# FFN activations turned in 32x32 blocks on VectorE and placed through DRAM, for ten of eleven blocks

## The chip, the cores and the metric

One NeuronCore of a Trainium2 chip runs the whole program. The metric is the device time of one execution in microseconds (us). A core has a tensor engine (PE, with its weight loads PEld), VectorE (DVE), ScalarE (ACT), GpSimd (POOL) and SyncE (SP), which here issues every DMA. Each engine takes its instructions in the order in which they were written for it, and waits at the first one that is not ready.

## The reference

The reference is a two-layer decoder trunk on 256 tokens of 1024 features, in float32. In each layer a feed-forward network (FFN) stands before and behind a mixer, so there are four FFNs:

```python
def swiglu(h, w_gate, w_up, w_down):
    return (jax.nn.silu(h @ w_gate) * (h @ w_up)) @ w_down

def rms_norm(x, gain):
    xf = x.astype(jnp.float32)
    y = xf * lax.rsqrt(jnp.mean(xf * xf, axis=-1, keepdims=True) + RMS_EPS)
    return (y * gain.astype(jnp.float32)).astype(x.dtype)

for layer in range(DEPTH):
    x = x + 0.5 * swiglu(rms_norm(x, ffn1_norm[layer]), ffn1_w_gate[layer], ffn1_w_up[layer], ffn1_w_down[layer])
    h = rms_norm(x, mix_norm[layer])
...
    x = x + mix
    x = x + 0.5 * swiglu(rms_norm(x, ffn2_norm[layer]), ffn2_w_gate[layer], ffn2_w_up[layer], ffn2_w_down[layer])
...
```

w_gate and w_up are 1024 x 2816, w_down is 2816 x 1024. The mixer of layer 0 is an mLSTM beside cross-attention to a memory, that of layer 1 a dilated attention beside the same; between the layers one projection makes the keys and values that layer 1 uses. The change touches the FFNs alone.

## The kernel before

**Numbers.** Each float32 matrix is held as two float32r parts, hi (rounded) and lo (what that leaves), and each product is three matmuls (`mm3`, lines 555 to 560): the low part of the weights by the high part of the activations first, then high by high, then high weights by the low part of the activations.

**Weights.** They come as one stream of units of [128, 1024] floats (512 KB), in the order of use. SP loads a unit into one of six tiles `raw`; ACT rounds it to `hi` (1024 columns); DVE subtracts to get `lo`; both go into a ring of eight units. So the load of unit i waits for the `lo` of unit i-6 (line 499), and the `hi` of unit i waits until PE has done with unit i-8 (line 508). In the names below raw221 is unit 221.

**An FFN** (`ffn`, lines 720 to 783) cuts the 2816 hidden features into eleven blocks of 256 (b = 0 to 10), and the tokens into two tiles of 128 (t = 0, 1). `gu(b, t)` multiplies the tokens by four units of gate and up weights: 24 matmuls of 512 columns into a bank of PSUM, `gups`. Each quarter of them uses one unit, and the unit's place in the ring is free when the same quarter of t = 1 is done. Then a side chain, `hidden(b, t)`, makes the activations: `sil` on ACT, `h` [128 tokens, 256] on DVE, two transposes on PE (128x128 each, by an identity, into the PSUM tile `tph`), `hh` on ACT and `hl` on DVE (hi and lo of the transposed tile). `dn(b, t)` multiplies `hh`, `hl` by two units of down weights, 12 matmuls, into four banks `acc` that stay open over all blocks.

**The order.** PE runs gu(0,0), gu(0,1), gu(1,0), gu(1,1), dn(0,0), dn(0,1), gu(2,0), gu(2,1), dn(1,0), dn(1,1) and so on, one block behind, up to dn(7); the end is gu(9,0), gu(9,1), gu(10,0), dn(8,0), gu(10,1), dn(9,0), dn(10,0), dn(8,1), dn(9,1), dn(10,1). This main stream is fixed by the loops. Where the side chains and the splits of the weights are put between it, on PE, ACT, DVE and SP, is decided when the program is written out: `_Model` (lines 168 to 263) keeps a clock for each engine by rough costs, and a chain's next step is written when that clock says that its inputs are ready. The costs are constants of the code, for a DMA a time by size and 2.0 us until it lands. On the chip the written order is all that is left of this.

Of the kernel before, what the change touches and what calls it, by code (L numbers as in the profile page):

```python
# [8 lines left out]
F32 = mybir.dt.float32  # L9
# [8 lines left out]
P = 128  # L18
# [4 lines left out]
NB = FF // FB  # L23
EPS = 1e-6
# [19 lines left out]
def kper(layer, which, b):  # L44
    return 1 if (layer, which, b) == (0, 1, 0) else 2


def _stream():
    """The weights in the order in which they are used: (key, source, slices, width)."""
# [64 lines left out]
def _pack(units, w):  # L114
    """Lay the weights out as one flat array, unit after unit, [128, width] each."""
    parts = []
    for _, src, _ in units:
        if src is None:
            continue
        name, index, cols, k, n = src  # L120
        if cols is None:
            a = w[name][index] if index is not None else w[name]
            parts.append(a[k * P:(k + 1) * P, :].reshape(-1))
# [18 lines left out]
def _consts():  # L142
    """Constants of the shapes alone: identity, triangle, ones, selectors, T5 buckets, masks."""
# [122 lines left out]
class _Engine:  # L266
    """An engine of the core whose instructions the model follows."""
# [57 lines left out]
class _Chain:  # L325
    """A chain of steps that is emitted beside the main stream, each when the one before is done."""
# [6 lines left out]
class _Kernel:  # L333
# [74 lines left out]
    def until(self, t):  # L408
        """run the chains that are ready before the main stream can go on at t"""
# [19 lines left out]
    def wait(self, *chains):  # L429
        """in a chain: until others are done"""  # L430
# [5 lines left out]
    def when(self, *aps):  # L436
        """in a chain: until something is written"""
# [3 lines left out]
    def psum(self, pool, shape, name):  # L441
        """in a chain: a bank of PSUM, once no more than can be are held by chains"""
# [30 lines left out]
    def emit_unit(self):  # L473
        """the next unit's steps begin: hi, the weights in float32r, and lo, what that leaves"""
# [24 lines left out]
    def loads(self):  # L499
        """loads run as far ahead of the splits as there are tiles"""  # L500
# [7 lines left out]
    def unit_ready(self):  # L508
        """when the split of the next unit can begin without delaying other work"""
# [57 lines left out]
    def rpow(self, ss, n, scale):  # L567
        """(ss * scale + eps) ** -0.5, [128, n]"""
# [7 lines left out]
    def rms(self, src, out, later=LATER):  # L576
        """out [128, 1] = 1 / rms of each row of src [128, 1024]"""
# [12 lines left out]
    def transposed(self, src, hi, lo, chunks, gain=None):  # L590
        """hi, lo [128, 8, 128] take the transposed 128-column chunks of src, times the gain"""
# [46 lines left out]
    def head_norm(self, src, n, out, rstd):  # L638
        """out = src * rstd normed over groups of 64; src [128, n*64] in PSUM"""
# [29 lines left out]
    def memory_load(self, layer):  # L669
        """the memory, ahead of its use"""  # L670
# [18 lines left out]
    def project(self, ps, x, key, n, kper):  # L689
        """ps [128, n] = xT.T @ weights of the block; x is xT or the number of a tile of tokens"""  # L690
# [13 lines left out]
    def block(self, x, key, n, kper, after):  # L704
        """a block of n columns of a projection; after(ps) are the steps that take it on"""
# [13 lines left out]

    def ffn(self, layer, which, after):  # L720
        nc = self.nc
        acc = [[self.acc.tile([P, 512], F32, tag="acc", name=f"acc{t}{h}") for h in range(2)]
               for t in range(2)]
        chains, hT = {}, {}

        def hidden(b, t):
            def steps(ps):
                yield from self.wait(self.stats[t])
                rstd = self.rstd[t]
                sil = self.work.tile([P, FB], F32, tag="ta", bufs=4, name="sil")  # L730
                nc.scalar.activation(sil, ps[:, :FB], AF.Silu, scale=rstd)
                yield
                h = self.work.tile([P, FB], F32, tag="ta", bufs=4, name="h")
                nc.vector.scalar_tensor_tensor(h, ps[:, FB:], rstd, sil, ALU.mult, ALU.mult)
                yield FREE
# [8 lines left out]
                hT[b, t] = (hh, hl)  # L744
            return steps

        def gu(b, t):
            chains[b, t] = self.block(t, ("gu", layer, which, b), 512, kper(layer, which, b), hidden(b, t))

        def dn(b, t):  # L750
            self.finish(chains.pop((b, t)))
            hh, hl = hT.pop((b, t))
# [3 lines left out]
            for n, (c, h) in enumerate(pairs):  # L756
                wh, wl = self.get("dn", layer, which, b, c)
                self.until(max(self.model.ready(a) for a in (wl, hl)))
                s = slice(c * P, (c + 1) * P)
                f = slice(h * 512, (h + 1) * 512)  # L760
                self.mm3(acc[t][h], (hh[:, s], hl[:, s]), (wh[:, f], wl[:, f]),
# [106 lines left out]
    def out_part(self, key, t, acc, haT, order, chunks, after=None):  # L868
        """some chunks of an output projection; the last ones end with the residual"""
# [21 lines left out]

    def mixer_a(self, after):
        nc, io = self.nc, self.io
        with ExitStack() as ctx:
# [44 lines left out]
            def gates():  # L939
                # u = i - cumsum(log sigmoid f), cg = max(0, running max of u)  # L940
# [210 lines left out]

    def shared_kv(self, again):
# [298 lines left out]
```

## Time and profile before

| what | value |
|---|---|
| median of three timed runs | 1037.3 us (1035.68 to 1037.99) |
| profiled execution, first to last instruction (span) | 1036.0 us |
| PE busy | 1019.0 us, 98% of the span |
| DVE busy, ACT busy | 616.1 us (59%), 557.5 us (54%) |
| moved by DMA | 182.53 MB, the main queue busy 52.0% |
| transposes of FFN activations (`tph`) | 176, 272 ns each |

The profiled execution is told by its span alone; the timed runs are executions of their own, and their median is 1.3 us above it. In the views, L545 is a matmul of the helper `matmul`, L552 a transpose, and L276 stands for every instruction of the other engines. Times in a row are us from the start of the span. `<-` behind an idle time names what ended it. A matmul's duration (about 390 ns) overlaps the next one's; the time that it costs is the distance from start to start.

### The profile page before, as it was taken

How to read it: one execution, taken by the hardware profiler on the slowest of the kernel's cores; microseconds unless marked ns; L12 is line 12 of the kernel's file. 1: busy time of each engine (PE TensorE's matmuls, PEld its weight loads, DVE VectorE, ACT ScalarE, POOL GpSimd, SP SyncE). 2: the span in 40 equal slices, each digit the busy share in tenths (PEclk: the TensorE clock that was granted, in tenths of full speed). 3: DMA queues.
4: the chain of work that ended last, by engine and by line, in shares of the span. 5: the costliest groups of instructions: out<-in, count | busy, mean ns of one | idle time of the engine just before them, and what ended most of it. 6: DMA issues, size and time to landing. Idle time of an engine off the chain costs nothing.

```text
span 1036.0 us, 13199 instructions
## 1 busy us (share of the span) xinstructions
PE 1019.0 (98%) x4888; PEld 840.4 (81%) x4888; DVE 616.1 (59%) x903; ACT 557.5 (54%) x913; POOL 43.7 (4%) x78
## 2 busy tenths in 40 slices
PE   7999999999999999999999999999999999999998
PEld 5888888898888888888877888888887688888886
DVE  6655554767866755554565755455476865545452
ACT  7544453596775744454466644445366774545441
POOL 0000000111110000000011000000003000000000
PEclk9999999999999999999999999999999999999999
DMA  8764644553537465656454656464552246555531
GB/s 292 246 212 166 214 166 152 169 196 103 185 104 241 146 215 169 209 166 211 164 188 163 208 199 207 167 214 166 181 198 68 82 167 218 170 198 184 182 121 41
DMA packets 54329, 182.53 MB, mean 176 GB/s; under 512 B 6332, under 2 KB 8180, under 8 KB 54264
## 3 DMA queue, kind: packets, MB, share of 16 engines
q1 hardware_dynamic: 54264, 181.69, 52.0%
q8 instruction: 38, 0.62, 0.2%
q14 instruction: 27, 0.22, 0.1%
HBM read 180.60 MB, written 1.07 MB: 175 GB/s over the span
## 4 chain that ended last, share of the span: by engine, by line
PE 92%; DVE 3%; ACT 2%; DMA 1%; issue 1%; POOL 0%; SPq 0%; DVEq 0%; ACTq 0%
PE gups L545 47%; PE acc L545 23%; PE aps L545 6%; PE oacc L545 3%; PE bqps L545 2%; PE mkvps L545 2%; PE kvps L545 2%; PE tph L552 2%; PE tps L552 2%; DVE lo L276 1%; DMA raw<-in_wts 1%; PE sc L545 1%; DVE s L276 1%; PE ms L545 1%; PE po L545 0%
## 5 line engine op out<-in xcount | busy, mean ns | idle before, releaser
L276 DVE TENSOR_TENSOR lo<-raw,hi 128x1024 fp32r<-128x1024 f32 (+3 forms) x347 | 404.1, 1184 | 152.0 <-ACT hi L276 137.2
L276 ACT CAST hi<-raw 128x1024 fp32r<-128x1024 f32 (+3 forms) x347 | 349.3, 1021 | 110.7 <-PE acc L545 66.0
L545 PE MATMUL gups<-lo,xh 128*128 128x512 f32 x704 | 280.9, 399 | 1.3 <-DVE lo L276 1.3
L545 PE MATMUL gups<-hi,xl 128*128 128x512 f32 x704 | 275.8, 392 | 0.0
L545 PE MATMUL gups<-hi,xh 128*128 128x512 f32 x704 | 275.1, 391 | 0.0
L545 PEld LDWEIGHTS gups<-hi,xl 128*128 128x128 f32 x704 | 132.6, 188 | 28.5
L545 PEld LDWEIGHTS gups<-lo,xh 128*128 128x128 f32 x704 | 132.6, 188 | 28.5 <-DVE lo L276 2.9
L545 PEld LDWEIGHTS gups<-hi,xh 128*128 128x128 f32 x704 | 133.0, 189 | 25.9
L545 PE MATMUL acc<-lo,hh 128*128 128x512 f32 x352 | 141.8, 403 | 0.0
L545 PE MATMUL acc<-hi,hl 128*128 128x512 f32 x352 | 138.0, 392 | 0.0
L276 ACT ACTIVATE sil<-gups,rstd 128x256 f32<-128x256 f32 x88 | 41.8, 475 | 178.3 <-PE gups L545 178.3
L545 PE MATMUL acc<-hi,hh 128*128 128x512 f32 x352 | 137.2, 390 | 0.0
L276 DVE SCALAR_TENSOR_TENSOR h<-gups,rstd,sil 128x256 f32<-128x256 f32 x88 | 42.3, 481 | 140.9 <-ACT sil L276 140.9
L545 PEld LDWEIGHTS acc<-hi,hl 128*128 128x128 f32 x352 | 66.1, 188 | 14.5
L545 PEld LDWEIGHTS acc<-hi,hh 128*128 128x128 f32 x352 | 66.4, 189 | 12.6
L276 ACT CAST hh<-tph 128x256 fp32r<-128x256 f32 x88 | 32.8, 372 | 80.9 <-PE tph L552 80.9
L545 PEld LDWEIGHTS acc<-lo,hh 128*128 128x128 f32 x352 | 66.2, 188 | 12.2
L276 DVE TENSOR_TENSOR hl<-tph,hh 128x256 fp32r<-128x256 f32 x88 | 37.4, 425 | 39.7 <-ACT hh L276 39.7
L545 PE MATMUL aps<-lo,xh 128*128 128x384 f32 (+1 forms) x144 | 49.8, 346 | 0.0
L545 PE MATMUL aps<-hi,xl 128*128 128x384 f32 (+1 forms) x144 | 47.6, 330 | 0.0
L545 PE MATMUL aps<-hi,xh 128*128 128x384 f32 (+1 forms) x144 | 47.5, 330 | 0.0
L276 ACT ACTIVATE xh<-tps,gains 128x128 fp32r<-128x128 f32 x112 | 31.9, 373 | 24.8 <-PE tps L552 24.8
(176 smaller groups left out, 932.8 us busy)
## 6 DMA issues: line engine op xcount, KB each, us to landing
raw<-in_wts SPq DMA_DIRECT2D x304, 512.0 KB, 4.6
raw<-in_wts SPq DMA_DIRECT2D x32, 384.0 KB, 3.6
raw<-in_wts SPq DMA_DIRECT2D x8, 256.0 KB, 4.6
mt<-in_mem SPq DMA_DIRECT2D x4, 512.0 KB, 5.8
bias<-diag SPq DMA_DIRECT2D x1, 1536.0 KB, 8.0
x<-in_x SPq DMA_DIRECT2D x4, 256.0 KB, 3.6
out<-x SPq DMA_DIRECT2D x4, 256.0 KB, 2.0
raw<-in_wts SPq DMA_DIRECT2D x2, 396.0 KB, 3.5
```

Of the source, the lines that this page charges most:

```text
L276: call(out, *args, **kw)
L545: self.pe.matmul(out, lhsT=lhsT, rhs=rhs, start=start, stop=stop)
L552: self.pe.transpose(out, in_, ident)
```

## The change

For blocks 0 to 9 of each FFN (`TURNED = NB - 1` is 10) the activations are no longer transposed on PE. DVE turns `h` [128, 256] (made as before, by `activated`) in 32x32 blocks with one instruction for each t, into a tile `hb` [128, 512] that holds both token tiles. When both are there, SP writes `hb` to a DRAM tile `hd` (256 KB, runs of 2 KB), and reads it back as `ht` [128, 512], with four runs of 512 bytes for each partition, so that each 32x32 block lands where the full transpose has it. One ACT instruction and one DVE instruction, 512 columns each, split `ht` into `hhb` and `hlb`, in place of two of 256 columns each. The features land on the partitions in another order (32 j + r on 4 r + j), and the rows of the down weights of these blocks are laid out in that order on the host. Block 10 stays on PE.

```diff
+TURNED = NB - 1
     def dn(b):
         for c in range(2):
-            units.append((("dn", layer, which, b, c), (d, layer, None, 2 * b + c, 1), D))
+            rows = "turned" if b < TURNED else None
+            units.append((("dn", layer, which, b, c), (d, layer, rows, 2 * b + c, 1), D))
...
+            if cols:
+                a = a.reshape(4, 32, -1).transpose(1, 0, 2)
...
+    def hidden_blocks(b, t):
+        def steps(ps):
+            h = self.work.tile([P, FB], F32, tag="ta", bufs=4, name="h")
+            yield from activated(ps, t, h)
+            if t == 0:
+                blocks[b] = fp.tile([P, 4, 2, 2, 32], F32, tag="hb", bufs=2, name="hb")
+            nc.vector.transpose(blocks[b][:, :, :, t, :].rearrange("p j c t -> p c j t"),
+                                h.rearrange("p (c j e) -> p c j e", c=2, j=4))
+        return steps
+
+    def placed(b, before):
+        yield from self.wait(*before)
+        hb = blocks.pop(b)
+        d = self.dram.tile([P, 512], F32, tag="hd", bufs=3, name="hd")
+        nc.sync.dma_start(d, hb.rearrange("p j c t e -> p (j c t e)"))
+        yield
+        ht = fp.tile([P, 4, P], F32, tag="ht", bufs=2, name="ht")
+        nc.sync.dma_start(ht, bass.AP(d.tensor, d.offset, [[P, P], [32 * 512, 4], [1, P]]))
+        yield
+        hh = fp.tile([P, 4, 4, 32], F32R, tag="hh", bufs=3, name="hhb")
+        hl = fp.tile([P, 4, 4, 32], F32R, tag="hl", bufs=3, name="hlb")
+        yield from self.split(*(a.rearrange("p c i e -> p i c e") for a in (hh, hl)),
+                              ht.rearrange("p i (c e) -> p i c e", c=4))
...
     def gu(b, t):
-        chains[b, t] = self.block(t, ("gu", layer, which, b), 512, kper(layer, which, b), hidden(b, t))
+        steps = hidden_blocks if b < TURNED else hidden
+        chains[b, t] = self.block(t, ("gu", layer, which, b), 512, kper(layer, which, b),
+                                  steps(b, t))
+        if b < TURNED and t == 1:
+            chains[b, 0] = chains[b, 1] = self.spawn(placed(b, [chains[b, 0], chains[b, 1]]))
```

The matmuls and their order on PE stay; 160 of the 176 transposes `tph` are gone from between them. The change also moves what the planner writes around them.

SP's queue in the third FFN (layer 1, first), where block 0 is handed over; before, it holds weight loads alone:

```order
L276 DMA raw220_5497<-in_wts 128x1024
L276 DMA raw221_5552<-in_wts 128x1024
L276 DMA raw222_5561<-in_wts 128x1024
L276 DMA raw223_5573<-in_wts 128x1024
L276 DMA raw224_5592<-in_wts 128x1024
```

The same place with the change (hd_5449 and ht_5497 are the write and the read of block 0, hd_5519 and ht_5546 those of block 1):

```order
L281 DMA raw220_5443<-in_wts 128x1024
L281 DMA hd_5449<-hb_5402 128x512
L281 DMA raw221_5486<-in_wts 128x1024
L281 DMA ht_5497<-hd_5449 128x4x128
L281 DMA raw222_5500<-in_wts 128x1024
L281 DMA raw223_5512<-in_wts 128x1024
L281 DMA hd_5519<-hb_5474 128x512
L281 DMA raw224_5529<-in_wts 128x1024
L281 DMA ht_5546<-hd_5519 128x4x128
```

The read of block 0 stands behind the load of unit 221, which waits for the `lo` of unit 215. The second and the fourth FFN have the same rows there. From the third block on, the write follows the load that the `lo` behind `h` frees, and two weight loads stand between write and read.

ACT's queue at that place before, from `sil` of gu(0,1) to the splits behind `sil` of gu(1,1):

```order
L276 ACTIVATE sil_5479<-gups_5421,rstd_4826 128x256
L276 CAST hi214_5485<-raw214_5404 128x1024
L276 CAST hh_5502<-tph_5499 128x256
L276 ACTIVATE sil_5521<-gups_5481,rstd_4734 128x256
L276 CAST hh_5535<-tph_5532 128x256
L276 CAST hi215_5538<-raw215_5426 128x1024
L276 CAST hi216_5554<-raw216_5432 128x1024
L276 CAST hi217_5566<-raw217_5446 128x1024
L276 ACTIVATE sil_5575<-gups_5523,rstd_4826 128x256
L276 CAST hi218_5580<-raw218_5464 128x1024
```

ACT's queue there with the change:

```order
L281 ACTIVATE sil_5426<-gups_5373,rstd_4773 128x256
L281 CAST hi214_5436<-raw214_5355 128x1024
L281 ACTIVATE sil_5464<-gups_5428,rstd_4681 128x256
L281 CAST hi215_5479<-raw215_5378 128x1024
L281 CAST hi216_5491<-raw216_5384 128x1024
L281 CAST hi217_5505<-raw217_5397 128x1024
L281 ACTIVATE sil_5515<-gups_5466,rstd_4773 128x256
L281 CAST hhb_5521<-ht_5497 128x4x4x32
L281 CAST hi218_5525<-raw218_5411 128x1024
```

The two `hh` of block 0 stood ahead of hi215; the one `hhb` of block 0 stands behind the last `sil` of block 1. Unit 215 takes the ring place of unit 207, the first unit of gu(1).

SP's queue in the first FFN before, at the same stage:

```order
L276 DMA raw20_362<-in_wts 128x1024
L276 DMA raw21_384<-in_wts 128x1024
L276 DMA raw22_413<-in_wts 128x1024
L276 DMA raw23_426<-in_wts 128x1024
L276 DMA raw24_438<-in_wts 128x1024
L276 DMA raw25_457<-in_wts 128x1024
```

And with the change:

```order
L281 DMA raw20_360<-in_wts 128x1024
L281 DMA hd_363<-hb_283 128x512
L281 DMA raw21_378<-in_wts 128x1024
L281 DMA raw22_403<-in_wts 128x1024
L281 DMA raw23_415<-in_wts 128x1024
L281 DMA raw24_427<-in_wts 128x1024
L281 DMA ht_433<-hd_363 128x4x128
L281 DMA hd_436<-hb_397 128x512
L281 DMA ht_445<-hd_436 128x4x128
L281 DMA raw25_448<-in_wts 128x1024
```

Here the read of block 0 has moved behind the load of unit 24, which waits for the `lo` of unit 18; unit 18 takes the place of unit 10, the third unit of gu(1) (units 8 to 11).

More of the change, by code (lines that the diff above doesn't have):

```diff
@@ L120, in _pack @@
         name, index, cols, k, n = src
-        if cols is None:
+        if cols is None or cols == "turned":
             a = w[name][index] if index is not None else w[name]
-            parts.append(a[k * P:(k + 1) * P, :].reshape(-1))
+            a = a[k * P:(k + 1) * P, :]
+            if cols:
+                a = a.reshape(4, 32, -1).transpose(1, 0, 2)
+            parts.append(a.reshape(-1))
             continue
@@ L720, in ffn, with ffn_in @@
     def ffn(self, layer, which, after):
+        with ExitStack() as ctx:
+            self.ffn_in(layer, which, after, self.pool(ctx, f"ffn{layer}{which}"))
+    def ffn_in(self, layer, which, after, fp):
         nc = self.nc
@@ L723, in ffn, with activated @@
                for t in range(2)]
-        chains, hT = {}, {}
+        chains, hT, blocks = {}, {}, {}
+        def activated(ps, t, out):
+            yield from self.wait(self.stats[t])
+            rstd = self.rstd[t]
+            sil = self.work.tile([P, FB], F32, tag="ta", bufs=4, name="sil")
+            nc.scalar.activation(sil, ps[:, :FB], AF.Silu, scale=rstd)
+            yield
+            nc.vector.scalar_tensor_tensor(out, ps[:, FB:], rstd, sil, ALU.mult, ALU.mult)
+            yield FREE
         def hidden(b, t):
             def steps(ps):
[L728 to L732, printed above, removed]
                 h = self.work.tile([P, FB], F32, tag="ta", bufs=4, name="h")
-                nc.vector.scalar_tensor_tensor(h, ps[:, FB:], rstd, sil, ALU.mult, ALU.mult)
-                yield FREE
+                yield from activated(ps, t, h)
                 tp = yield from self.psum("tp", [P, 512], "tph")
@@ L757, in dn @@
                 wh, wl = self.get("dn", layer, which, b, c)
-                self.until(max(self.model.ready(a) for a in (wl, hl)))
-                s = slice(c * P, (c + 1) * P)
+                self.until(max(self.model.ready(a) for a in (wl, parts[c][1])))
                 f = slice(h * 512, (h + 1) * 512)
-                self.mm3(acc[t][h], (hh[:, s], hl[:, s]), (wh[:, f], wl[:, f]),
+                self.mm3(acc[t][h], parts[c], (wh[:, f], wl[:, f]),
                          b == 0 and c == 0, last and c == 1)
```

9 lines of the change are left out of this document (7 added, 2 removed).

## The prediction

> **What bounds the kernel now.** I read the page first, then the groups by form, then the chain of waits.
>
> ```profile
> span 1036.0 us, 13199 instructions
> PE 1019.0 (98%) x4888; PEld 840.4 (81%) x4888; DVE 616.1 (59%) x903; ACT 557.5 (54%) x913; POOL 43.7 (4%) x78
> PE 92%; DVE 3%; ACT 2%; DMA 1%; issue 1%; POOL 0%; SPq 0%; DVEq 0%; ACTq 0%
> ```
>
> PE is busy for nearly the whole span and carries 92% of the chain that ends last. DVE and ACT have two fifths of the span to spare. So a matmul slot freed on PE is time gained, unless PE then waits. The groups that the change touches, and those that price its new work:
>
> ```profile
> L552 PE MATMUL tph<-consts,h 128*128 128x128 f32 x176 | 33.5, 272 | 0.0
> L276 ACT CAST hi<-raw 128x1024 fp32r<-128x1024 f32 x304 | 316.8, 1052 | 106.7 <-PE acc L545 64.8 <-PE gups L545 25.0 <-PE oacc L545 8.7
> L276 DVE TENSOR_TENSOR lo<-raw,hi 128x1024 fp32r<-128x1024 f32 x304 | 366.6, 1224 | 143.7 <-ACT hi L276 129.0
> L276 ACT CAST hi<-raw 128x512 fp32r<-128x512 f32 x8 | 4.6, 634 | 0.0
> L276 DVE TENSOR_TENSOR lo<-raw,hi 128x512 fp32r<-128x512 f32 x8 | 5.2, 686 | 1.0 <-ACT hi L276 1.0
> ```
>
> The second row shows that the splits of the weights wait for PE to free a place in the ring, and for no load: weights lie ready. In the chain, one period of a block (two tiles of `gu`, two of `dn`) in the first FFN:
>
> ```profile
> 52.26 2.04 PE acc L545 x9
> 54.30 0.22 PE tph L552 x2
> 54.52 3.45 PE acc L545 x15
> 57.97 6.80 PE gups L545 x30
> 64.77 0.22 PE tph L552 x2
> 64.99 4.11 PE gups L545 x18
> 69.10 2.04 PE acc L545 x9
> ```
>
> From 52.26 to 69.10 is 16.84 us without a gap, for 72 matmuls and two pairs of transposes. The stretches that no transposes precede run at 0.2267 us a matmul (6.80 / 30, 2.04 / 9).
>
> **Removed: the transposes on PE.** 72 matmuls at 0.2267 are 16.32 us, so a pair costs (16.84 - 16.32) / 2 = 0.26 us: 0.22 in the chain, and some 0.04 in the matmuls behind it (15 in 3.45 us are 0.230 each). Ten blocks, two token tiles, four FFNs are 80 pairs: 80 x 0.26 = **-20.8 us**. If only the chain's 0.22 goes, it is -17.6.
>
> **Added on DVE and ACT.** For each block two turns on DVE; the trace has no such instruction, and its bounds are the 128x1024 `lo` (1.22 us) and nothing; I take 0.5 us, near DVE's other 128x256 forms. The split of 512 columns costs 0.63 on ACT and 0.69 on DVE. A period has 16.3 us and these engines idle for over 40% of it, so the work itself costs nothing; its place in the queues counts.
>
> **Added on SP: 80 DMAs, with a wait in its queue.** The read of a block waits for the landing of its write, and every weight load behind it waits too. Those loads have room:
>
> ```profile
> SPq L276 <- DVE lo L276: 779.9, 323, 11.6
> ```
>
> SP stands 780 us of the span waiting for `lo` to free a raw tile, six units ahead. A stop of a few us for each block costs nothing there, and 40 x 0.5 MB beside 182.53 MB fit in queues that are half idle. Without that room each stop would fall on PE.
>
> What a placed block waits for is the read's landing. Prices for it (issue to landing), in order: a weight load alone (issued at 59 us), three in a row (33 to 36.6 us), the one write to the outside, the one strided read from DRAM:
>
> ```profile
> raw<-in_wts SPq DMA_DIRECT2D x1, 512.0 KB, 3.5
> ...
> raw<-in_wts SPq DMA_DIRECT2D x3, 512.0 KB, 5.3
> ...
> out<-x SPq DMA_DIRECT2D x4, 256.0 KB, 2.0
> bias<-diag SPq DMA_DIRECT2D x1, 1536.0 KB, 8.0
> ```
>
> The last row, less 2.0, is 6.0 us for 1536 KB, so 1.0 us for 256 KB (an estimate); its runs are 1 KB, and at 512 bytes it may be 2.0; at best the read hides in the load ahead (0). I take 1.0, the nearest row as it stands. The Trainium skill ("DMA: Bandwidth & Descriptors", Specifications) gives 512 bytes as the smallest transfer at full rate; by that the 1.0 stands, and the 2.0 falls away.
>
> **The price at the head of each FFN.** Block 0 has a shorter way than the others: from the end of gu(0,1), only gu(1,0) and gu(1,1) run before dn(0,0) wants `hhb`. In the new order the read stands behind a weight load, which waits for the `lo` of a unit whose ring place gu(1,1) itself frees: in the second to fourth FFN its first quarter (unit 215 in the third), in the first FFN its third (unit 18). That third-quarter split, and dn(0,0), stand in the first FFN so:
>
> ```profile
> 34.07 1.05 ACT L276 CAST hi<-raw 128x1024 fp32r<-128x1024 f32 x1 [0.33 <-PE gups L545]
> ...
> 35.24 0.39 PE L545 MATMUL acc<-lo,hh 128*128 128x512 f32 x1
> ```
>
> So `hi` of a third-quarter place starts 1.17 us before dn(0,0) is due, and one of the first quarter, 12 matmuls earlier, 1.17 + 12 x 0.2267 = 3.89 before. The third matmul is the first that needs `hlb`, 0.45 later.
>
> From the start of that `hi`: `hi` 1.05 and `lo` 1.22, with handovers of some 0.1, and the load is issued at 2.35. The read behind it lands 3.5 + 1.0 later, at 6.85; `hhb` 0.63 and `hlb` 0.69 with handovers make it 8.25. Due was 3.89 + 0.45 = 4.34: PE waits 3.9 us. In the first FFN loads come in a row (5.3): 2.35 + 5.3 + 1.0 + 1.4 = 10.05 against 1.17 + 0.45 = 1.62: 8.4 us. Together 8.4 + 3 x 3.9 = **+20.1 us**. With the read hidden it is 16.1, with 2.0 us for it 24.1.
>
> **What a wait of PE brings after it.** The trace has one of 2.5 us:
>
> ```profile
> 531.75 0.39 PE L545 MATMUL kvps<-hi,xl 128*128 128x512 f32 x1
> 534.62 0.80 PE L545 MATMUL pb<-hot,rel 32*12 32x384 f32 x2 [2.49 <-DMA raw<-in_wts]
> ...
> 537.07 0.63 PE L545 MATMUL kvps<-hi,xl 128*128 128x512 f32 x1
> 537.50 0.63 PE L545 MATMUL kvps<-lo,xh 128*128 128x512 f32 x1
> ...
> 536.00:539.00 3.00, 3.00 (x9) 2.33 (x8) 0.69 (x2) 0.69 (x1) 0.90 (x2) 0.51 0.15 28
> ```
>
> From 536 to 539 us the granted clock (third figure from the right) is 0.51 and matmuls are 0.43 us apart, not 0.227: 8 of them lose 8 x 0.2 = 1.6 us. Four waits longer than this one cost 4 x 1.6 = **+6.4 us**; bounds 0 and twice that. The Trainium skill ("TensorE: Matmul & The Clock Gate", What's actually happening) says that the clock falls after a whole idle window of about 3.4 us; here a shorter wait was enough, so I go by the row, and the page's rule is a rival below.
>
> **Steady blocks.** From the end of gu(b,1), dn(b-1) and gu(b+1) run, 16.3 us, before dn(b,0). The read follows the second load that dn(b-1,1) frees. The usual landing of a load (issue to landing), and the rows of that place:
>
> ```profile
> raw<-in_wts SPq DMA_DIRECT2D x304, 512.0 KB, 4.6
> ```
>
> ```profile
> 58.00 1.06 ACT L276 CAST hi<-raw 128x1024 fp32r<-128x1024 f32 x1 [0.31 <-PE acc L545]
> ...
> 66.38 3.71 DVE L276 TENSOR_TENSOR lo<-raw,hi 128x1024 fp32r<-128x1024 f32 x3 [0.52 <-ACT hi L276]
> ```
>
> Its load goes at 58.0 + 2.35 = 60.35; with 4.6 and 1.0 the read lands at 65.95. `hhb` is done at 66.6, `hlb` after the first of those `lo` (67.6) at 68.3; dn(b,0) is due near 69.1 - 0.5, its third matmul at 69.05. It fits by 0.75 us, and the read may land 1.3 us later, since `hlb` waits for that `lo` anyway. Cost: 0. The end of an FFN has 13.6 us and a read straight behind its write: 0 as well.
>
> **The sum.** 1036.0 - 20.8 + 20.1 + 6.4 = 1041.7 us of span, and the median of the runs lies 1.3 above the profiled span: **1043.0 us**. A measurement of this kernel tells about 0.2% (2.1 us) from no change: under 1035.2 is faster, over 1039.4 slower.
>
> **Rivals.**
>
> 1. *The clock stays up* except where the idle time is longer than a window of 3.4 us for certain, the first head: 1043.0 - 3 x 1.6 = 1038.2 us, no change that can be measured. This is a mechanism of PE's activity counter: 3.9 us of idle time need not hold one whole window. For it: the page named above. Against: the wait of 2.5 us in the trace. Chance 0.17.
>
> 2. *The reads pass the loads.* If the small read shares the 16 queues with the load ahead and lands with it, the waits are 2.9 and 7.4, 16.1 in sum; short waits may also leave the clock up: 1036.0 + 1.3 - 20.8 + 16.1 = 1032.6 us, faster. If the planner's place for block 0 did no harm at all, it would be 1016.5. For it: SP's queue is nearly idle there, one load in flight. Against: the order puts the load's issue, not its transfer, at 2.35 of 4.34 us. Chance 0.15.
>
> 3. *Placement binds in every block.* The steady margin of 1.3 us is thin. If the 512-byte runs or the write's landing add 2.3 us more than I took, each of some 32 blocks waits 1.0 us: 1043.0 + 32 = 1075 us. It decides from a read that lands more than 6.9 us after the load ahead is issued (4.6 + 1.0 + 1.3). For it: the longest chain of DMAs in the program has no spare. Against: a load behind another lands in 4.5 to 5.3. Chance 0.1.
>
> That the transposes do not go is no rival: the new order has 16 of 176.
>
> **How the numbers follow.** The main case has 0.58 and a range of its own of 1036 to 1051: landing 0 to 2.0 us gives -4.0 to +4.0, the clock -6.4 to +6.4, the smaller gain +3.2, not all at once. Rival 1 lies inside it; the range reaches down to the upper form of rival 2 and up over part of rival 3: 1032 to 1058. Faster: rival 2 with 0.15, and 0.03 of the main case's low end. Same: 0.10 of rival 1 and 0.07 of the main case. Slower: the rest, 0.65.
>
> **What would show it.** Right: in the chain of the profile after, steady periods of 16.3 us; before the first `acc` of each FFN an idle PE, ended by DVE `hlb` or ACT `hhb`, of about 8 us once and 4 us three times; a granted clock near 0.5 in the 3 us behind each. ACT's wait before `hhb` is put down to the DMA `ht`. Wrong: periods still at 16.8 (the transposes cost nothing or placement eats them, rival 3), or no idle PE at the heads (rival 2), or a clock of 1.0 behind them (rival 1). If DVE's turn takes well over 1.2 us, my bound on it falls, though it lies on no path that I found.

## The result, and the profile after

| | median of four runs | ratio to before, 95% interval |
|---|---|---|
| before | 1036.9 us (1035.68 to 1037.99) | |
| with the change | 1047.0 us (1045.17 to 1049.62) | 1.0097 (1.0080 to 1.0114) |

Slower by 10 us; the forecast was 1043.0 with 1032 to 1058. The profiled execution of the changed kernel has a span of 1047.9 us, the longest of its four runs; its excess over before, 11.9 us, is what is taken apart here.

The page of the changed kernel: the totals, the chain that ended last, and the two new transfers (KB each, and the median time from issue to landing). In the views from here on L550 (L551 or L552 in some runs) is the matmul of the helper, and L281 stands for every instruction of the other engines.

```profile
span 1047.9 us, 13123 instructions
PE 1012.3 (97%) x4728; PEld 833.5 (80%) x4728; DVE 636.6 (61%) x943; ACT 550.8 (53%) x873; POOL 45.0 (4%) x78
PE 89%; DVE 3%; ACT 3%; DMA 3%; issue 1%; POOL 0%; SPq 0%; DVEq 0%; ACTq 0%
hd<-hb SPq DMA_DIRECT2D x40, 256.0 KB, 5.5
ht<-hd SPq DMA_DIRECT2D x40, 256.0 KB, 4.6
```

160 matmuls fewer, and yet PE's busy time falls by 6.7 us only: some of those that are left got longer. The chain has 3% of DMA now, 1% before. The two places to look at are those that the prediction named: the head of each FFN and the steady blocks. First a head, that of the third FFN, in the chain of waits:

```profile
609.20 1.06 ACT hi L281
...
610.29 1.24 DVE lo L281
...
611.92 4.04 DMA ht<-hd
...
615.99 0.63 ACT hhb L281
...
616.65 8.47 PE acc L550 x24
```

From `hi` of the unit whose place gu(1,1) frees, through its `lo`, the load's issue, the read of block 0 and `hhb`: the chain leaves PE at 609.2 and comes back to it at 616.65, exactly the steps of the prediction. The 24 matmuls of dn(0) then take 8.47 us instead of 5.4. Why they do is seen on PE's own timeline at the fourth head, and in the granted clock there (third figure from the right):

```profile
882.78 0.79 PE L550 MATMUL acc<-lo,hhb 128*128 128x512 f32 x1 [3.38 <-ACT hhb L281]
883.38 0.63 PE L550 MATMUL acc<-hi,hhb 128*128 128x512 f32 x1
883.80 0.63 PE L550 MATMUL acc<-hi,hlb 128*128 128x512 f32 x1
```

```profile
882.00:885.00 3.00, 2.22 (x5) 1.77 (x6) 1.92 (x2) 1.56 (x2) 0.00 (x0) 0.50 0.89 317
885.00:888.00 3.00, 3.00 (x8) 2.31 (x7) 0.00 (x0) 0.00 (x0) 0.00 (x0) 0.50 0.71 235
```

Behind 3.4 us of idle time the clock stands at 0.50 for some six us, and a matmul costs 0.43 us. From the starts of PE's matmuls in the trace, the wait (less one slot of 0.2267) and what the 72 matmuls behind it take over 72 x 0.2267:

| FFN | wait at the head | lost behind it |
|---|---|---|
| first | 8.35 | 2.81 |
| second | 3.67 | 2.04 |
| third | 3.57 | 2.88 |
| fourth | 3.55 | 2.86 |
| sum | 19.1 | 10.6 |

All stretches of this trace at the low clock from 15 us to the end of PE's work, the third of them in a mixer (on both sides of each the clock is 1.00):

```profile
38.74:48.98 10.24, 5.71 (x13) 4.42 (x14) 2.61 (x3) 2.18 (x3) 0.00 (x0) 0.50 0.56 182
373.25:376.66 3.41, 3.41 (x10) 2.64 (x9) 0.60 (x1) 0.00 (x0) 0.00 (x0) 0.50 0.73 255
543.92:547.32 3.40, 3.40 (x9) 2.64 (x9) 0.96 (x2) 1.59 (x2) 1.86 (x2) 0.50 0.45 90
615.59:622.42 6.83, 5.76 (x14) 4.47 (x15) 1.92 (x2) 1.56 (x2) 0.00 (x0) 0.50 0.77 255
881.83:888.66 6.83, 5.88 (x14) 4.58 (x15) 1.92 (x2) 1.56 (x2) 0.00 (x0) 0.50 0.77 263
```

They last 3.4 us or two or three times that, and they don't begin with the wait: at the second head PE starts again at 371.74, and its clock falls at 373.25. The stretch in the mixer follows an idle time of 1.36 us and two small matmuls (the kernel before has its own there, from 536.07 to 539.49, so it makes next to no difference between the two).

Next the steady blocks, a period in the first FFN and one in the second (chain of waits):

```profile
62.57 5.44 PE acc L550 x24
68.01 10.88 PE gups L550 x48
```

```profile
406.78 5.60 PE acc L550 x24
412.38 10.91 PE gups L550 x48
```

In the first, 5.44 + 10.88 is 16.32 us, the 72 x 0.2267 of the prediction, where before had 16.84 to 16.87. In the second FFN, and the third, `dn` takes 5.60: each of its matmuls is 0.2333 us behind the last. No engine waits there; that is a loss that nobody had foreseen (0.16 us a block).

### The profile page after: what moved, and what is told of

The parts are those of the page before. It is cut to its first block, busy times and chain, and to the rows that moved or that the text cites. A ratio compares the mean times of both kernels' runs of the same rounds, so it can differ in the third digit from the quotient of the medians.

```text
span 1047.9 us, 13123 instructions
## 1 busy us (share of the span) xinstructions
PE 1012.3 (97%) x4728; PEld 833.5 (80%) x4728; DVE 636.6 (61%) x943; ACT 550.8 (53%) x873; POOL 45.0 (4%) x78
## 4 chain that ended last, share of the span: by engine, by line
PE 89%; DVE 3%; ACT 3%; DMA 3%; issue 1%; POOL 0%; SPq 0%; DVEq 0%; ACTq 0%
PE gups L550 45%; PE acc L550 23%; PE aps L550 6%; PE oacc L550 3%; PE mkvps L550 2%; PE bqps L550 2%; DVE lo L281 1%; PE tps L557 1%; DMA ht<-hd 1%; ACT hi L281 1%; PE kvps L550 1%; PE sc L550 1%; DVE s L281 1%; DMA hot<-in_consts 1%; PE ms L550 1%
## 5 line engine op out<-in xcount | busy, mean ns | idle before, releaser
L281 DVE TENSOR_TENSOR lo<-raw,hi 128x1024 fp32r<-128x1024 f32 (+3 forms) x347 | 403.9, 1182 | 165.4 <-ACT hi L281 159.5
L281 ACT CAST hi<-raw 128x1024 fp32r<-128x1024 f32 (+3 forms) x347 | 347.1, 1020 | 174.0 <-PE acc L550 108.4
L550 PE MATMUL gups<-lo,xh 128*128 128x512 f32 x704 | 275.7, 392 | 1.3 <-DVE lo L281 1.3
L550 PE MATMUL gups<-hi,xl 128*128 128x512 f32 x704 | 274.9, 390 | 0.0
L550 PE MATMUL gups<-hi,xh 128*128 128x512 f32 x704 | 274.8, 390 | 0.0
L550 PEld LDWEIGHTS gups<-lo,xh 128*128 128x128 f32 x704 | 132.5, 188 | 30.1 <-DVE lo L281 2.7
L550 PEld LDWEIGHTS gups<-hi,xl 128*128 128x128 f32 x704 | 132.6, 188 | 27.7
L550 PEld LDWEIGHTS gups<-hi,xh 128*128 128x128 f32 x704 | 132.6, 188 | 27.5
L550 PE MATMUL acc<-lo,hhb 128*128 128x512 f32 x320 | 131.5, 411 | 18.5 <-ACT hhb L281 15.0
L281 ACT ACTIVATE sil<-gups,rstd 128x256 f32<-128x256 f32 x88 | 41.8, 475 | 180.3 <-PE gups L550 175.4
L550 PE MATMUL acc<-hi,hlb 128*128 128x512 f32 x320 | 129.2, 404 | 0.0
L550 PE MATMUL acc<-hi,hhb 128*128 128x512 f32 x320 | 129.0, 403 | 0.0
L281 DVE SCALAR_TENSOR_TENSOR h<-gups,rstd,sil 128x256 f32<-128x256 f32 x88 | 42.3, 480 | 137.5 <-ACT sil L281 137.5
L550 PEld LDWEIGHTS acc<-lo,hhb 128*128 128x128 f32 x320 | 62.5, 195 | 33.2 <-ACT hhb L281 16.3
L550 PEld LDWEIGHTS acc<-hi,hlb 128*128 128x128 f32 x320 | 62.1, 194 | 15.3 <-DVE hlb L281 1.1
L550 PEld LDWEIGHTS acc<-hi,hhb 128*128 128x128 f32 x320 | 62.7, 196 | 13.5
L550 PE MATMUL aps<-lo,xh 128*128 128x384 f32 (+1 forms) x144 | 49.7, 345 | 0.0
L550 PE MATMUL aps<-hi,xl 128*128 128x384 f32 (+1 forms) x144 | 47.5, 330 | 0.0
L550 PE MATMUL aps<-hi,xh 128*128 128x384 f32 (+1 forms) x144 | 47.5, 330 | 0.0
L281 ACT ACTIVATE xh<-tps,gains 128x128 fp32r<-128x128 f32 x112 | 32.0, 373 | 24.6 <-PE tps L557 24.6
L281 DVE SCALAR_TENSOR_TENSOR xl<-tps,gains,xh 128x128 fp32r<-128x128 f32 x112 | 31.3, 343 | 20.0 <-ACT xh L281 20.0
L281 ACT CAST hhb<-ht 128x512 fp32r<-128x512 f32 x40 | 24.8, 620 | 26.2 <-DMA ht<-hd 25.7
```

The costliest lines, as they stand in the source:

```text
L281: call(out, *args, **kw)
L550: self.pe.matmul(out, lhsT=lhsT, rhs=rhs, start=start, stop=stop)
```

## Experiments

All times are medians beside runs of the kernel before on the same chip (1036.4 to 1037.7 there).

| run | us | ratio to before, 95% interval |
|---|---|---|
| e1 block 0 on PE | 1019.5 | 0.9839 (0.9826 to 0.9853) |
| e2 read at once | 1032.6 | 0.9960 (0.9948 to 0.9973) |
| e3 other queue | 1095.0 | 1.0556 (1.0528 to 1.0583) |
| e4 filled wait | 1038.9 | 1.0024 (1.0014 to 1.0033) |
| e5 addresses | 1048.0 (one run) | |
| e6 block 0 on PE, addresses | 1022.7 | 0.9847 (0.9824 to 0.9870) |
| e7 other queue, same order | 1050.9 | 1.0113 (1.0074 to 1.0152) |
| e8 second hop | 1085.8 | 1.0466 (1.0419 to 1.0512) |
| e9 same address class | 1017.6 | 0.9813 (0.9793 to 0.9834) |
| e10 loads held | 1032.4 | 0.9954 (0.9936 to 0.9972) |
| e11 loads held, hhb first | 1035.6 | 0.9988 (0.9977 to 0.9999) |
| e12 all shifted | 1017.9 | 0.9817 (0.9797 to 0.9837) |

**Is it all at the heads? (e1)**

```diff
-            steps = hidden_blocks if b < TURNED else hidden
+            steps = hidden_blocks if 0 < b < TURNED else hidden
```

(and so for the two other tests of `b < TURNED`)

> Block 0 of each FFN is transposed on PE as before the change, blocks 1 to 9 stay turned. Theory A (all of the loss sits at block 0): the four waits (8.35 + 3.66 + 3.57 + 3.54 = 19.1 us in the trace after) and the slow matmuls behind them (about 10.5) go, and eight pairs of transposes at 0.27 come back (2.2): 1047.0 - 29.6 + 2.2 = 1019.6 us. Rival B (the first block that is turned waits, whichever it is): block 1 has 16.3 us instead of 10.9 from the end of its gu, so it would still miss by some of the 3.6: an idle PE before dn(1,0) and 1030 us or more.

Measured: 1019.5 us, 17 under before. The head of the fourth FFN in its chain:

```profile
854.94 0.23 PE gups L550
855.17 5.44 PE acc L550 x24
```

No wait, no slow matmul, and none at block 1 either: rival B falls. Nine turned blocks are a gain; the tenth, block 0, costs more than all of it.

**The clock (e4).** PE is given work in the wait.

```diff
+                if b == 0 and t == 0 and n == 0:
+                    xh = self.xT[0][0]
+                    for _ in range(33 if (layer, which) == (0, 1) else 13):
+                        self.pe.matmul(acc[0][0], lhsT=xh[:, 0, :],
+                                       rhs=xh[:, :4, :].rearrange("p a b -> p (a b)"),
+                                       start=True, stop=True)
                 self.mm3(acc[t][h], parts[c], (wh[:, f], wl[:, f]),
```

> PE gets 33 matmuls of 512 columns to do in the wait of the first FFN, and 13 in each of the other three; they write the bank that dn(0,0) then starts anew, so the result is not touched. Everything else stands as in the changed kernel. Theory A (the matmuls behind a wait are slow because PE was idle and its granted clock fell to 0.5): the waits stay, PE's pace behind them is 0.227 us a matmul, and about 10.5 us go: 1036.5 us. Rival B (they are slow because the loads and splits that had piled up run beside them, or because of the tiles they read): the pace stays at 0.43 for some 6 us, 1047 us.

Measured: 1038.9 us, 8.1 less than the changed kernel. The waits are about those of the changed kernel (7.48 in the first FFN, which is just what the 33 matmuls take, then 3.69, 3.58 and 3.63 us), and 0.4 to 0.5 us is lost behind each instead of 2.0 to 2.9. The windows at the fourth head:

```profile
872.00:875.00 3.00, 2.48 (x10) 1.46 (x9) 1.49 (x2) 1.57 (x2) 0.00 (x0) 1.00 0.92 303
875.00:878.00 3.00, 3.00 (x15) 2.45 (x14) 0.43 (x1) 0.04 (x1) 0.00 (x0) 1.00 0.81 261
```

The clock stays at 1.00 beside the same DMA share (0.92 and 0.81, where it was 0.89 and 0.71) and the same splits. So the slow matmuls come of the idle time, and of nothing that runs beside them.

**The order on SP (e2).** Block 0's read stands directly behind its write.

```diff
             nc.sync.dma_start(d, hb.rearrange("p j c t e -> p (j c t e)"))
-            yield
+            if b:
+                yield
             ht = fp.tile([P, 4, P], F32, tag="ht", bufs=2, name="ht")
```

> For block 0 alone the read ht is written into SP's queue directly behind the write hd, ahead of the weight load that stood between. Theory A (order: the read waits for a load that waits for lo, and then shares the queue with it): the read is issued when the write lands, 0.95 us sooner in the second and fourth FFN, and has no load ahead of it; hhb is then held by ACT's order (it stands behind sil of gu(1,1)), some 1.3 us after dn(0,0) is due. Waits of 1.3 to 2.1 instead of 3.6 and about 6 instead of 8.35: 1047.0 - 8 = 1039 us if the clock still falls, 1029 if it doesn't. Rival B (length: write, landing, read and split take some 10.5 us in any order): only the 0.95 is won, four times, 1043 us, with waits of 2.6 and 7.4.

Measured: 1032.6 us, 14 less than the changed kernel, between the two numbers of theory A. The waits are 5.14, 1.32, 1.68 and 1.63 us. The chain at the fourth head:

```profile
857.13 5.43 DMA hd<-hb
...
862.58 2.99 DMA ht<-hd
...
866.26 6.01 PE acc L550 x24
```

The load is gone from the chain, and the read, with no load ahead of it, takes 2.99 instead of 4.0. In its place stands the write: 5.43 us for 256 KB. And the waits of 1.3 to 1.7 us do not bring the clock down: at the second head,

```profile
363.00:366.00 3.00, 1.84 (x9) 1.08 (x7) 2.76 (x3) 2.25 (x4) 0.00 (x0) 1.00 0.94 272
366.00:369.00 3.00, 3.00 (x13) 2.30 (x13) 2.13 (x4) 0.74 (x1) 0.00 (x0) 1.00 0.85 303
```

the clock is 1.00 in and behind it, and 0.4 to 0.55 us is lost there.

**What holds the write: its queue? (e3, e7)** In both, GpSimd issues write and read; the planner keeps a clock of its own for GpSimd in e3 (shown below), and in e7 counts them as SP's, so that all else is written in the order of the changed kernel.

```diff
-            nc.sync.dma_start(d, hb.rearrange("p j c t e -> p (j c t e)"))
+            nc.gpsimd.dma_start(d, hb.rearrange("p j c t e -> p (j c t e)"))
```

> Write and read of every turned block are issued by GpSimd in a queue of its own; SP has weight loads alone. Theory A (the write lands 5.4 us after its issue because it stands behind a 512 KB load in one queue): here it lands in about 3 us, the read too, and the waits at the heads fall to what ACT's order leaves, 1.3 us, and 3 to 5 in the first FFN: 1047.0 - 3 x 2.3 - 4 = 1036 us with the clock still falling, 1026 without. Rival B (a write to DRAM and a read back take this long by themselves): landings stay at 5 us, waits stay, 1047 us. Rival C: GpSimd's queue is slower to start than SP's, and blocks 1 to 9 wait as well: over 1050.

Measured: 1095.0 us, the worst of all, as rival C had it, but not for its reason. The waits of ACT, in this run and then in the changed kernel:

```profile
ACT hhb L281 <- DMA ht<-hd: 330.0, 39, 10.9
```

```profile
ACT hhb L281 <- DMA ht<-hd: 25.7, 25, 7.0
```

The planner, for which a read by GpSimd doesn't stand behind the weight loads, wrote `hhb` ahead of the splits of the weights; ACT stood 330 us at `hhb`, with the splits queued behind it. So e3 can't tell what a queue of its own is worth; e7 was made for that.

> Write and read of the turned blocks are issued by GpSimd, and everything else stands in the order of the changed kernel, ACT and DVE included (in the run with the other queue the splits hhb had moved ahead on ACT too). Theory A (the read at the heads is held by the weight load ahead of it in SP's queue, the write by the bytes of the loads in flight, in whatever queue): the read is issued when the write lands, 0.95 us sooner, and lands in 3.3 instead of 4.1; GpSimd's issue takes 0.8 more for both: waits of about 2.6 in three FFNs, about 7.5 in the first, steady blocks without a wait: 1043 us. Rival B (the write is held by the load ahead of it in its own queue): it lands in 3 us, and the waits fall to the 1.3 that ACT's order leaves: 1030 us. Rival C (GpSimd's way is slow whatever the order of ACT): steady blocks wait as in the run before, 1095 us.

Measured: 1050.9 us, no different from the changed kernel (the intervals of the ratios overlap), with waits of 8.16, 3.60, 6.47 and 3.94 us and no wait in steady blocks. The write in its own queue, issue to landing:

```profile
hd<-hb POOLq DMA_DIRECT2D x40, 256.0 KB, 5.2
```

Rival B falls: the write is as late in a queue of its own. Rival C falls too. So does theory A's sum: counted from the end of gu(1,1), the read of the second FFN was issued 0.7 us sooner than in the changed kernel (365.71 and 366.92 in the two traces, whose gu(1,1) end at 367.61 and 368.08) and landed no sooner, 2.9 us behind that end in both: beside the loads it took 4.8 us instead of 4.1.

**What holds the write: the loads in flight? (e10)**

```diff
     def loads(self):
-        while self.loaded < len(self.units) and len(self.raw) + len(self.running) < RAW:
+        while not self.hold and self.loaded < len(self.units) and \
+                len(self.raw) + len(self.running) < RAW:
```

(`hold` is set ahead of gu(0,1) and taken back behind the read of block 0, in the second to fourth FFN; the read stands at once behind the write as in e2)

> All ten blocks turned, block 0's read directly behind its write in SP's queue as in the run with the read at once, and in the second to fourth FFN the four weight loads that the planner puts between the middle of gu(0,1) and that read are written behind it. Theory A (the write lands 5.1 us after its issue because the bytes of loads in flight stand before it): it lands in 2.5, the read in 2.9, before gu(1,1) ends, and hhb is held by ACT's order alone, behind sil of gu(1,1): waits of 1.3 us in those three FFNs (after the read at once they are 1.3, 1.7 and 1.6), 5.1 in the first; 1032.6 - 1 = 1031.6 us. Rival B (5 us are the way itself): waits of 1.3 to 1.7 as before, landings of 5 us. Rival C (the weights held back come too late): hi of units 133 to 136 waits for its load, and PE in gu(2,0): some us each, 1040.

Measured: 1032.4 us. The issues around the second head, and ACT there:

```profile
hd<-hb SPq DMA_DIRECT2D x1, 256.0 KB, 2.0
```

```profile
364.55 0.47 ACT L281 ACTIVATE sil<-gups,rstd 128x256 f32<-128x256 f32 x1 [1.66 <-PE gups L551]
364.93 0.61 ACT L281 CAST hhb<-ht 128x512 fp32r<-128x512 f32 x1
```

With no load in flight the same 256 KB land in 2.0 us instead of 5.4, at all three heads. The waits are 1.28, 1.23 and 1.23, and no transfer holds them now: `hhb` stands behind `sil` of gu(1,1), which PE releases only when gu(1,1) ends. Both parts of theory A are borne out; the time is that of e2, because a second limit lay just below the first. The Trainium skill ("DMA: Bandwidth & Descriptors", Queues, rings and completion order) says that the signal of a DMA's completion lands only after every earlier write of the same DMA engine, in whatever queue. By that a queue of its own can't help and fewer loads in flight do; e7 and e10 agree, though no run separates the late signal from late data.

**Both limits away (e11).** As e10, and `sil` of gu(1,1) waits until the planner has written `hhb` of block 0.

```diff
                 h = self.work.tile([P, FB], F32, tag="ta", bufs=4, name="h")
+                if (b, t) == (1, 1):
+                    yield from self.wait(first[0])
                 yield from activated(ps, t, h)
```

> As the run with the loads held, and on ACT sil of gu(1,1) is written behind hhb of block 0 instead of ahead of it. Theory A (with loads out of the way and ACT's order turned, the way from gu(0,1) to dn(0,0) fits in 10.9 us): no wait at the second to fourth heads, 1031.6 - 3 x (1.3 + 0.4) = 1026.5 us; the first FFN still waits 5 us with the slow clock behind it. Rival B (the landings take 5 and 3 us whatever stands beside them): waits of 1.3 to 1.7 as before, 1032 us.

Measured: no wait at the three heads, as theory A said, but 1035.6 us. The loss turns up one block later; the third FFN's ACT, with dn(1,0) due at 616.8:

```profile
605.22 1.05 ACT L281 CAST hi<-raw 128x1024 fp32r<-128x1024 f32 x1 [0.24 <-DMA raw<-in_wts]
606.18 0.46 ACT L281 ACTIVATE sil<-gups,rstd 128x256 f32<-128x256 f32 x1
...
623.58 0.62 ACT L281 CAST hhb<-ht 128x512 fp32r<-128x512 f32 x1 [6.08 <-DMA ht<-hd]
```

`sil` of gu(1,1) now stands behind splits that wait for the loads held back (PE had been done with gu(1,1) at 600.3), the write of block 1 goes out 9.1 us behind the end of gu(1,1), in e10 1.7, and PE waits 7.4 us before dn(1,0) of that FFN. The way does fit in the 10.9 us between gu(0,1) and dn(0,0), but not without taking the time from others.

**The margin of the steady blocks (e8).** Block 0 on PE; one more copy, DRAM to DRAM, between write and read.

```diff
+            e = self.dram.tile([P, 512], F32, tag="he", bufs=3, name="he")
+            self.tc.nc.sync.dma_start(e, d)
+            d = e
             ht = fp.tile([P, 4, P], F32, tag="ht", bufs=2, name="ht")
```

> Block 0 on PE; blocks 1 to 9 are written to DRAM, copied there once more (256 KB), and read back: one landing more in the way. It puts a price on the margin of the steady blocks. In the trace after, hlb is done 1.4 us before its first use, hhb 2.0. Theory A (the margin is thin, and a later landing falls on PE): a hop of 3 to 5 us makes each of 36 blocks wait 1.5 to 3.5 us: 1019.5 + 54 to 126, some 1100 us. Rival B (the planner's late place for hhb hides it, or the waits of SP leave more room than the trace shows): under 1030 us.

Measured: 1085.8 us, 66 more than e1. The last two of the three transfers of a block, and one round of the chain of waits in the first FFN:

```profile
he<-hd SPq DMA_DIRECT2D x36, 256.0 KB, 3.6
ht<-he SPq DMA_DIRECT2D x36, 256.0 KB, 2.9
```

```profile
69.42 0.02 ACT hhb L281
...
71.94 0.37 ACT sil L281
...
75.36 4.70 DMA hd<-hb
...
80.08 3.87 DMA he<-hd
...
84.01 2.82 DMA ht<-he
...
86.86 0.02 ACT hhb L281
```

From the end of the turn to the start of `hhb` it is 11.9 us now (median of 36 blocks), 1.4 more than in e1. PE waits before 32 of the 36 blocks, 36 us in sum or 1.0 a block; most of the rest of the 66 us is matmuls that are slow, behind these waits or at the low clock. So the margin is thin, as theory A had it, but it isn't the margin of `hhb` alone: in ACT's queue `hhb` stands ahead of two splits and of the next block's `sil`, so a late read makes the next write late as well. The chain runs in a ring, from `hhb` to the next `hhb` in 17.44 us, where PE's own work for a block is 16.32.

**The 0.2333 us of the second and third FFN (e5, e6, e9, e12).** The tiles `hhb` and `hlb` belong to a pool of each FFN, which lies at another address in those two. An unused tile ahead of them moves them. In `dn`, `hhb` and `hlb` are the stationary operand of PE (loaded as weights, 128x128, ahead of each matmul) and the units `hi` and `lo` the moving one (512 columns that stream through).

```diff
         chains, hT, blocks = {}, {}, {}
+        fp.tile([P, {(0, 1): 8, (0, 2): 16, (1, 1): 8, (1, 2): 16}[layer, which]], F32,
+                tag="pad", bufs=1, name="pad")
```

> The changed kernel with a small unused tile ahead of the FFN's own tiles, so that hhb and hlb begin at byte 0, 96, 64 and 32 of 128 in the four FFNs, in this order; in the changed kernel they begin at 96, 32, 32 and 96. In its trace the matmuls of dn are 0.2333 us apart in the second and third FFN and 0.2267 in the first and fourth. Theory A (a tile at byte 32 of 128 as PE's stationary operand costs 0.0067 us a matmul): 0.2333 in the fourth FFN, 0.2267 in the second; the first and third show whether 0 and 64 are free of it. Rival B (the second and third FFN differ in something else, the traffic or the work beside them): 0.2333 in the second and third as before, whatever the address.

Measured: slow in all four. The fourth FFN, which had 5.44, and which nothing but 64 bytes tells from the changed kernel:

```profile
915.37 5.60 PE acc L550 x24
```

So the address does it (rival B falls), but 96 of 128 in the second FFN did not help: theory A's rule was wrong.

> Block 0 on PE as in the first experiment, and hhb and hlb at byte 0, 96, 64 and 0 of 128 in the four FFNs, 32 in none. Theory A (addresses): 18 blocks x 24 matmuls x 0.0067 us = 2.9 us less than block 0 on PE alone: 1019.5 - 2.9 = 1016.6 us. If byte 64 is slow as well, half of it: 1018. Rival B: 1019.5.

Here the addresses were still chosen by the rule of 128 bytes (the last FFN's tiles in fact start at 96 of 128, not at 0): 1022.7 us, slower than block 0 on PE alone, with 0.2333 in all four FFNs. The rule that fits all eight is the start within 256 bytes (e9: pads of 448 and 192 bytes in the second and third FFN, none in the others).

> Block 0 on PE. The last address run found 0.2333 us a matmul wherever hhb and hlb had been moved, byte 96 of 128 among them, and 0.2267 only where they lay unmoved. In the fast places (first and fourth FFN, and every other tile that PE reads with 0.2267) the start is 224 bytes behind a multiple of 256; in the slow ones it is 0, 32, 64 or 96 behind. Here the tiles of the second FFN start at 224 of 512, those of the third at 480 of 512 (both 224 of 256), the other two stay. Theory A (what counts is the start within 256 bytes): 0.2267 in all four FFNs, 1019.5 - 2.9 = 1016.6 us. Rival A' (within 512): 0.2267 in the second, 0.2333 in the third, 1018 us. Rival B (it is something else in those FFNs, or any tile of padding slows it): 0.2333 in both, 1019.5 us.

Measured: 1017.6 us, and the second FFN's chain:

```profile
374.80 5.44 PE acc L551 x24
```

All four FFNs run at 0.2267 us: theory A. The gain over e1, 1.9 us, is within what the two intervals leave open; e6 and e9, which differ in this alone but ran on two chips, are 5.1 us apart (3.5 by their ratios, whose intervals just overlap), where 36 blocks x 24 x 0.0067 would make 5.8. What bears the argument is the pace in the traces, not these times. Last, 64 bytes ahead of everything (e12):

```diff
+        self.const.tile([P, 16], F32, tag="pad", bufs=1, name="pad0")
         self.keep = pool("keep")
```

> As the run with the same address class, but an unused tile of 64 bytes ahead of everything shifts all tiles at once: the weights (hi, lo), the activations of gu (xh, xl), hhb and hlb all start 32 bytes behind a multiple of 256 now, where 224 was before. Theory A (what counts is that the stationary tile and the moving tile lie alike within 256 bytes): 0.2267 us a matmul everywhere, 1017.6 us. Rival B (what counts is the byte itself: 32 is slow as in the second and third FFN of the changed kernel, 224 is fast): 0.2333 us for all of some 4500 matmuls, gu's too: 1017.6 + 4500 x 0.0067 = 1047 us.

Measured: 1017.9 us, 0.2267 everywhere. The byte itself doesn't matter. What fits all runs is that stationary and moving tile must start alike within 256 bytes; the tiles `hb` and `ht` moved along with `hhb` and `hlb` each time, and no run moved the moving tile alone.

## Why the prediction was right, and where its sizes were off

- **Removed transposes: right.** 0.27 a pair in the first and fourth FFN (16.86 to 16.32 us a period, two pairs), 80 x 0.27 = -21.6 where -20.8 was forecast. What was missing is the price of the new tiles' addresses: 20 blocks x 24 x 0.0067 = +3.2. The prediction has no step for this effect.
- **DVE's and ACT's new work: right.** The turn, bounded by 0 and 1.22 and taken as 0.5 us, took 0.44, on no path that sets the end:

```profile
L281 DVE STREAM_TRANSPOSE hb<-h 128x256 f32<-128x256 f32 x80 | 35.4, 442 | 1.5
```

- **The heads: right, with one leg unseen.** Forecast 8.4 and three times 3.9, measured 8.35 and 3.55 to 3.67; the chain goes through the very steps named, and the prices held: the load ahead of the read landed 3.6 us after its issue in the third FFN and the read 0.8 behind it (3.5 and 1.0 were taken), in the first 5.7 and 0.8 (5.3 and 1.0). The sum was worked out for `hlb`, and what PE waited for is `hhb`; by `hhb` the same terms give 6.85 + 0.63 - 3.89 = 3.6. But the write, which the working had left out, landed only 0.95 us ahead of the read's issue in the second FFN (issued 360.59, 5.4 us; the read at 366.92), as SP's own timeline shows:

```profile
360.59 0.37 SPq L281 DMA_DIRECT2D hd<-hb  x1
366.54 0.33 SPq L281 DMA_DIRECT2D raw<-in_wts  x1
366.92 0.43 SPq L281 DMA_DIRECT2D ht<-hd  x1
```

  Three limits lay within 2.4 us of each other: the load ahead of the read, the write behind the loads in flight, and `sil` ahead of `hhb`. The prediction priced the highest; e2, e10 and e11 laid the others bare one by one.
- **The clock behind a wait: right in kind, sized too small.** +6.4 was forecast, 1.6 for each wait from 8 slow matmuls in the one stretch of 3.4 us that the trace of before shows. At the second head the low clock lasted as long, and 2.04 was lost; at the others it lasted two or three times that, with some 13 slow matmuls. It makes 10.6 in sum, 10.3 without the 0.16 of the two slow FFNs, and is the largest error of the sum. The size varies from one execution to the next: in e5, with nearly the same waits (8.45, 3.76, 3.74, 3.46), three of the four low stretches are 3.4 us long and 8.5 is lost, and the three other executions of the changed kernel had a mean clock of 0.989 or 0.990 where the profiled one had 0.985. Rival 1 (the clock stays up at 3.6 us) falls: it fell at all four heads, and e4 shows that idle time alone does it.
- **Steady blocks: right, but by luck in part.** None waits. The working was another: the read is issued when its write lands (SP waits 42.4 us for that, 34 times), not when the second load is out of the way. For block 2, `hhb`, `hlb` and the matmuls that want them:

```profile
76.06 0.62 ACT L281 CAST hhb<-ht 128x512 fp32r<-128x512 f32 x1 [0.16 <-DMA ht<-hd]
```

```profile
77.07 0.68 DVE L281 TENSOR_TENSOR hlb<-ht,hhb 128x512 fp32r<-128x512 f32 x1
```

```profile
78.72 0.39 PE L550 MATMUL acc<-lo,hhb 128*128 128x512 f32 x1
...
79.18 0.39 PE L550 MATMUL acc<-hi,hlb 128*128 128x512 f32 x1
```

  The margin is 2.0 for `hhb` and 1.4 for `hlb`, where 0.75 to 1.3 was worked out. In e8 a way 1.4 us longer was enough to make nearly every block wait, so rival 3 was near.
- **The sum**, by the measured terms: 1036.0 - 21.6 + 3.2 + 19.1 + 10.3 = 1047.0; the profiled span is 1047.9. Of the rest 0.2 lies in the first 21 us, where PE waits for its first inputs in both kernels; the remainder isn't traced. Against the 1041.7 us of span that were forecast this is 6.2 more: 3.9 by the clock, 3.2 by the addresses and the rest of 0.9, less 1.0 at the heads and 0.8 by the transposes. The medians lie only 4.0 apart (1043.0 and 1047.0), as the profiled execution is the longest of its four. Rival 2 did not come: the reads do not pass the loads by themselves. Where one is let past (e2), the time is what that rival had worked out, 1032.6 us, but by chance: the waits are others (9.8 us instead of 16.1), and the clock stayed up three times only.

## What to carry to other kernels

Work that is taken off the bounding engine and sent through DRAM pays where the result has a full period to arrive, and loses where a pipeline starts: here nine of ten blocks were worth 17 us and the first one cost 27. Price a first iteration apart, with the wait and with the slow clock behind it, and leave it on the old path (e1, and with the tiles' addresses put right e9, beat both kernels: 1017.6 us). When the step named as the bound is removed and little is won, look at once for the next one behind it, and for who gets its time taken.

## What the runs showed of the hardware

- A matmul of 128x512 float32r costs 0.2267 us from start to start when stationary and moving tile start at the same byte within 256, and 0.2333 where they start 32, 64, 96 or 128 bytes apart in it (distances of 0 and 256 were fast). Why is open.
- A 256 KB write to DRAM lands 2.0 us after its issue with nothing in flight, and 5.2 to 5.5 beside weight loads, in their queue or in another.
- Idle times of PE of 1.2 to 1.5 us at three heads of e2 left the granted clock at 1.00 (0.4 to 0.55 us lost behind them); 3.4 us in the changed kernel and 3.3 in e5 brought it to 0.50, for 3.4 us or a multiple of it. The length of the idle time alone doesn't decide: 1.36 us in the mixer of the changed kernel, with two small matmuls behind it, was enough. The Trainium skill ("TensorE: Matmul & The Clock Gate", What's actually happening) puts the fall at a whole idle window of about 3.4 us. The length of the low stretches agrees with such a window, and so does the first head, idle for 8.2 us; that the window must be idle as a whole does not, for the 2.5 us wait in the kernel before and the 1.36 us were followed by a clock of 0.51 and 0.50.
